# A two-layer encoder trunk on eight cores: LayerNorm by token tile under a contraction-outer head of the second pointwise projection, later relayout reads, and ten modulation blocks moved to the first FFN

## The chip, the cores and the metric

The kernel runs on the eight cores of one Trainium2 chip (two dies: cores 0 to 3 and 4 to 7). Every core does the same work on its own slice of the tokens (1184 columns), so every core streams all the weights. The metric is the device time of the slowest core, in microseconds (us). The time before the change is 3435.83 us (median of 3 runs, 3432.84 to 3686.82).

The highest of those three is not scatter. In some executions of any version of this program, the cores of one die (or of both) show a lower granted TensorE clock and take longer. Such runs are called slow here, the others fast, and only fast runs are compared.

A ratio below is the mean time of one kernel's fast runs over the mean time of the other's fast runs of the same rounds. The interval in brackets is the 95% interval. A verdict of faster or slower needs a difference of over 2%; it is unclear where the interval reaches across 2%.

## The reference, cut to what matters

```python
def conv_module(h, state, w_pw1, b_pw1, w_dw, b_dw, ln_g, ln_b, w_pw2, b_pw2):
    a, gt = jnp.split(h @ w_pw1 + b_pw1, 2, axis=-1)
    u = a * jax.nn.sigmoid(gt)                                   # GLU
    up = jnp.concatenate([state.astype(u.dtype), u], axis=1)
    z = lax.conv_general_dilated(up, w_dw[:, None, :]...) + b_dw # depthwise, width 31
    z = jax.nn.silu(layer_norm(z, ln_g, ln_b))                   # over the 2048 channels
    return z @ w_pw2 + b_pw2, up[:, T:]

def run_trunk(x, c, ...):
    for i in range(2):                       # layer 0: conv module, layer 1: window attention
        mod = jax.nn.silu(c) @ p['w_mod'][i] + p['b_mod'][i]
        sh1, sc1, g1, sh2, sc2, g2 = jnp.split(mod, 6, axis=-1)
        h = modulate(rms_norm(x, p['norm_mix'][i]), sh1, sc1)
        y = conv_module(...) or attention(...)
        x = x + g1[:, None, :] * y
        h = modulate(rms_norm(x, p['norm_ffn'][i]), sh2, sc2)
        x = x + g2[:, None, :] * swiglu(h, p['w_gu'][i], p['w_down'][i])
```

The six modulation vectors of a layer are 48 "mod blocks" of 256 columns: blocks 0 to 7 are `sh1`, 8 to 15 `sc1`, 16 to 23 `g1`, 24 to 31 `sh2`, 32 to 39 `sc2`, 40 to 47 `g2`. A mod block is a 1 MB weight block (2048 x 256 in bf16, cast from float32 on its way in) for 1 us of matmul work.

## The kernel before

All weights flow through a ring of four 1 MB slots in the order of one list, `plan`. A slot is refilled in strict order: block `i` only goes where block `i - 4` was, and only when that one is done.

```python
        for b in range(24, 32):
            wblock(f"mod0_{b}", wmod, b, KC)
        for b in range(8):
            wblock(f"pw2_{b}", wpw2, b, KC)
            for m in PW2M[b]:
                wblock(f"mod0_{m}", wmod, m, KC)
        # ... layer 1:
                wblock("q_0", wqkv, 0, KC)
                for b in range(16, 26):
                    wblock(f"mod1_{b}", wmod, 48 + b, KC)
                for b in range(1, 8):
                    wblock(f"q_{b}", wqkv, b, KC)
                    for x in range(2):
                        wblock(f"mod1_{24 + 2 * b + x}", wmod, 72 + 2 * b + x, KC)

        def ring_fill():
            while ring["next_pf"] < len(plan) and (ring["next_pf"] < NR or ring["next_pf"] - NR in ring["rel"]):
                ring_prefetch(ring["next_pf"])
                ring["next_pf"] += 1
```

The convolution needs another layout of its input than pw1 (the first pointwise projection) gives, and so does LayerNorm of the convolution's output. Both go through DRAM: write `ud`, read `ud`; write `zd`, read `zd`, all issued by SyncE (SP). SP works in program order, so a read that waits for its write holds up all that SP issues after it.

```python
                t_w = dma(SP, ud[c], US[:, c % 2, :], us_sem[c % 2])           # end of pw1 chunk c
                # ...
                SP.wait(t_w, vb_free[c % 2])
                vb_ready[c] = dma(SP, VB[:, c % 2, :, :], ud[c].rearrange(...), vb_sem[c % 2])
    # ... and in conv_chunk(c):
            t_w = dma(SP, zd[c].rearrange(...), ZS[:, b, :, :], zs_sem[b])
            # ...
            SP.wait(t_w)
            zc_ready[c] = dma(SP, ZC[:, c, :], zd[c], zc_sem[c])
```

Then come the statistics matmuls, eight mod blocks, LayerNorm on whole rows of 1184 tokens, chunk by chunk of the 16 channel chunks, and pw2 (the second pointwise projection) with its epilogue, with the contraction `k` innermost:

```python
        for cc in range(KC):
            DVE.emit(... ZC[:, cc, :] - MEAN)
            DVE.emit(... ZC[:, cc, :] * RSC)
            act(HB[:, cc, 32:1184]..., zv..., AF.Silu, scale=lg, bias=lb)      # cut
            xready0.append(dma(SP, X[:, cc, :], xv[:, cc, 32:NH], xr_sem[cc])) # x replaces z
    # proj_resid, for each of 16 output rows n and 3 token tiles t:
                        PE.wait(*bf[bk])                                       # bk: two banks in turn
                        for k in range(KC):
                            mm(PS[bk][:, 0:ncols], slot[:, k, 128 * h:128 * h + 128], rhs_of(k, xlo, ncols), ...)
                        ACT.wait(tp, tfree)
                        act(TMPE[...], PS[bk][...], AF.Identity, scale=g1, bias=G1B)   # cut
                        DVE.emit(... X[:, n, xlo:xlo + ncols] += TMPE[:, 0:ncols])
                        tfree = DVE.tick()
```

In attention the list puts ten mod blocks of layer 1 between `q_0` and `q_1`; they are used up while ScalarE computes the position bias, before the first scores.

The softmax here doesn't subtract the row's maximum and nothing guards it: scores larger than these inputs give would overflow.

## Time and profile before

The profile is of the slowest core, core 3. Its page starts with the span and the busy time of each engine and has, further on, the chain of waits followed back from the last instruction:

```profile
span 3435.6 us, 54718 instructions; the slowest of 8 cores (3396.2 to 3435.6 us)
...
PE 3001.0 (87%) x21988; PEld 1861.9 (54%) x21988; DVE 1136.0 (33%) x2591; ACT 717.0 (21%) x1321; POOL 187.3 (5%) x357
...
PE 74%; DMA 14%; DVE 4%; ACT 3%; issue 3%; SPq 1%; DVEq 0%; POOL 0%; ACTq 0%; POOLq 0%
```

TensorE (PE) is the limit, busy for 87% of the span. PE time by itself can't be cut by this change, so what counts are the stretches where PE stands still. The next view gives the busy time in chosen stretches of core 3: the stretch, its length, busy us of each engine with the number of instructions, the granted PE clock, the mean DMA share, GB/s.

```profile
core 3: us, PE busy (x) PEld busy (x) DVE busy (x) ACT busy (x) POOL busy (x), PEclk, DMA share, GB/s
165.00:517.00 352.00, 317.37 (x2352) 202.11 (x2352) 170.12 (x459) 45.85 (x66) 21.10 (x40) 0.95 0.79 155
...
553.00:604.00 51.00, 6.49 (x228) 6.17 (x225) 45.63 (x38) 33.07 (x40) 4.23 (x8) 0.52 0.98 187
...
1955.00:2047.00 92.00, 39.87 (x705) 28.42 (x706) 17.33 (x47) 35.02 (x32) 5.63 (x11) 0.65 0.64 115
2047.00:2225.00 178.00, 161.23 (x1760) 115.54 (x1760) 94.05 (x243) 93.38 (x193) 10.11 (x20) 0.93 0.67 127
```

Read the second column against the first. pw1 and the convolution (165 to 517) leave PE idle for 35 us; LayerNorm (553 to 604) leaves it idle for 44 of 51 us, while DVE is nearly full but the DMA engines (0.98) are full too; the start of attention (1955 to 2047) leaves it idle for 52 us. The list of all PE waits, by what ended them (us in total, times, longest):

```profile
PE ps L250 <- DMA RING<-wmod: 85.5, 20, 8.0
...
PE ps L250 <- DMA UBraw<-ud: 46.1, 5, 12.6
```

Single instructions of PE show where they are (start, length, what, and in brackets the idle time just before it and what ended it). The first is a convolution chunk waiting for its relayout read; the next is the first pw2 matmul, which waits for LayerNorm's output; the last two are waits for mod blocks in attention.

```profile
345.87 5.15 PE L250 MATMUL ps<-UBraw 128*128 128x156 bf16 x40 [12.64 <-DMA UBraw<-ud]
...
604.29 11.01 PE L250 MATMUL ps<-HBraw,RING 128*128 128x384 bf16 x48 [16.92 <-ACT HBraw L253]
...
2010.52 1.00 PE L250 MATMUL ps<-SCT,RING 128*128 128x3 bf16 x32 [8.05 <-DMA RING<-wmod]
...
2084.81 0.99 PE L250 MATMUL ps<-SCT,RING 128*128 128x3 bf16 x32 [2.75 <-DMA RING<-wmod]
```

Why a read comes late is seen in SP's own issues. Each line is one transfer handed over; SP is stuck between them:

```profile
276.23 0.38 SPq L245 DMA_DIRECT2D ud<-UBraw  x1
...
281.46 0.37 SPq L245 DMA_DIRECT2D UBraw<-ud  x1
281.93 0.52 SPq L245 DMA_DIRECT2D zd<-UBraw  x1
291.44 0.33 SPq L245 DMA_DIRECT2D Xraw<-zd  x1
291.88 0.76 SPq L245 DMA_DIRECT2D ud<-UBraw  x1
```

The write of `zd` at 281.93 has to land before its read is issued at 291.44, and only then does SP get to the next `ud` write at 291.88: two round trips through DRAM in one line.

A stage runs from the first PE matmul of one kind to the first of the next, read from each core's trace and averaged over the eight cores: pw1, statistics, pw2, FFN 0, the K and V projections, the first scores, the output projection wo, FFN 1. Before:

| stage (us, mean of 8 cores) | before |
|---|---|
| pw1 to statistics | 367.7 (358 to 382) |
| statistics to first pw2 matmul | 56.0 |
| pw2 to FFN 0 | 158.4 |
| FFN 0 to K/V | 1136.3 |
| K/V to first scores | 147.0 |
| first scores to wo | 224.3 |
| wo to FFN 1, and FFN 1 to the end | 129.3, 1035.2 |

### The profile page before, as it was taken

The numbers are of one execution on the slowest core, as the hardware profiler recorded it, in microseconds if no ns is written. First come the engines' busy times: TensorE is split into PE (matmuls) and PEld (weight loads), VectorE is DVE, ScalarE is ACT, GpSimd is POOL, SyncE is SP. The second block draws the span as 40 slices with busy tenths as digits, with TensorE's granted clock in tenths as the row PEclk, the third lists the DMA queues.
The fourth block names the chain that finished last, engine by engine and source line by source line (L and its number), as shares of the span: only waits on it lengthen the run. The fifth ranks groups of instructions, "written<-read, shape, count | busy, mean of one in ns | idle before, by whom it ended". The sixth has DMA issues, their size and how long they took to land.

```text
span 3435.6 us, 54718 instructions; the slowest of 8 cores (3396.2 to 3435.6 us)
## 1 busy us (share of the span) xinstructions
PE 3001.0 (87%) x21988; PEld 1861.9 (54%) x21988; DVE 1136.0 (33%) x2591; ACT 717.0 (21%) x1321; POOL 187.3 (5%) x357
## 2 busy tenths in 40 slices
PE   2298982998999999999999649889899999999996
PEld 0165652554556565555554336656566666666663
DVE  0344547123231413122134525542322222323136
ACT  2411114453000000000003635555300000000003
POOL 0000000000000000000000000000000000000000
PEclk9999995999999999999999869979899999999998
DMA  9787778953666565424245376654375353535343
GB/s 214 135 149 158 159 153 173 208 104 60 125 107 115 86 124 90 82 44 84 46 77 129 87 122 125 127 148 74 53 134 97 50 99 50 95 53 90 54 74 120
DMA packets 107111, 366.87 MB, mean 107 GB/s; under 512 B 31424, under 2 KB 51008, under 8 KB 77920
## 3 DMA queue, kind: packets, MB, share of 16 engines
q0 software_dynamic: 51024, 285.67, 47.8%
q1 hardware_dynamic: 55840, 77.70, 7.6%
q8 instruction: 180, 2.95, 0.4%
q14 instruction: 67, 0.55, 0.1%
HBM read 615.89 MB, written 33.78 MB: 189 GB/s over the span
## 4 chain that ended last, share of the span: by engine, by line
PE 74%; DMA 14%; DVE 4%; ACT 3%; issue 3%; SPq 1%; DVEq 0%; POOL 0%; ACTq 0%; POOLq 0%
PE ps L250 74%; DMA RING<-wmod 4%; DMA ud<-UBraw 3%; DMA zd<-UBraw 2%; DMA Xraw<-xT 1%; SPq L245 1%; ACT HBraw L253 1%; DMA RING<-wgu 1%; DMA UBraw<-ud 1%; DVE Xraw L884 1%; DVE Xraw L607 1%; DMA RING<-wpw 1%; ACT SCR L253 1%; DMA RING<-wqkv 1%; DVE UBraw L465 0%
## 5 line engine op out<-in xcount | busy, mean ns | idle before, releaser
L250 PE MATMUL ps<-HBraw,RING 128*128 128x352 bf16 (+2 forms) x11616 | 1944.2, 328 | 88.9 <-ACT HBraw L253 57.9
L250 PEld LDWEIGHTS ps<-HBraw,RING 128*128 128x128 bf16 x11616 | 1139.3, 99 | 823.6 <-issue 121.2
L250 PE MATMUL ps<-UBraw,RING 128*128 128x352 bf16 (+2 forms) x4992 | 812.5, 320 | 15.4 <-DVE UBraw L534 7.3
L250 PEld LDWEIGHTS ps<-UBraw,RING 128*128 128x128 bf16 x4992 | 472.7, 98 | 331.7 <-issue 65.1
L534 DVE TENSOR_TENSOR UBraw<-ps,SCR 128x352 bf16<-128x352 f32 (+2 forms) x264 | 144.0, 547 | 1170.9 <-PE ps L250 1166.9
L253 ACT ACTIVATE SCR<-ps 128x352 f32<-128x352 f32 (+2 forms) x264 | 126.8, 482 | 1812.6 <-PE ps L250 1812.6
L607 DVE SCALAR_TENSOR_TENSOR Xraw<-ps,MOD,Xraw 128x16 f32<-128x16 f32 (+3 forms) x960 | 395.3, 447 | 322.0 <-PE ps L250 321.9
L250 PE MATMUL ps<-SCT,RING 128*128 128x3 bf16 x3072 | 90.9, 165 | 131.0 <-DMA RING<-wmod 85.5
L250 PEld LDWEIGHTS ps<-SCT,RING 128*128 128x128 bf16 x3072 | 90.0, 98 | 144.1 <-issue 136.7
L250 PE MATMUL ps<-SCR,ONESB 128*128 128x352 bf16 (+2 forms) x240 | 80.0, 362 | 78.5 <-ACT SCR L253 78.5
L253 ACT ACTIVATE SCR<-Xraw 128x352 bf16<-128x352 f32 (+3 forms) x208 | 117.1, 565 | 120.6 <-DVE Xraw L511 66.9
L511 DVE TENSOR_TENSOR Xraw<-Xraw,SCR 128x352 f32<-128x352 f32 (+2 forms) x96 | 52.6, 548 | 221.2 <-ACT SCR L253 216.1
L253 ACT ACTIVATE Xraw<-Xraw 128x512 bf16<-128x512 f32 (+4 forms) x154 | 107.6, 720 | 51.8 <-DVE Xraw L1143 36.5
L245 POOL DMA_DIRECT2D RING<-wmod x96 | 50.9, 532 | 919.1 <-PE ps L250 806.6
L245 POOL DMA_DIRECT2D RING<-wdn x96 | 50.7, 528 | 891.5 <-PE ps L250 888.9
L250 PE MATMUL ps<-UBraw 128*128 128x156 bf16 x640 | 54.8, 254 | 48.5 <-DMA UBraw<-ud 46.1
L245 POOL DMA_DIRECT2D RING<-wgu x88 | 46.5, 529 | 888.1 <-PE ps L250 871.3
L253 ACT ACTIVATE SCR<-ps,G1B,MOD 128x16 f32<-128x16 f32 (+3 forms) x160 | 79.1, 536 | 75.8 <-PE ps L250 75.7
L1143 DVE SCALAR_TENSOR_TENSOR Xraw<-ps,Xraw 128x512 f32<-128x512 f32 x128 | 82.3, 685 | 36.1 <-PE ps L250 36.0
L250 PEld LDWEIGHTS ps<-SCR,ONESB 128*128 128x128 bf16 x240 | 23.2, 102 | 110.6 <-issue 102.5
L250 PEld LDWEIGHTS ps<-UBraw 128*128 128x128 bf16 x640 | 52.8, 109 | 51.8 <-issue 50.2
L745 DVE SCALAR_TENSOR_TENSOR UBraw<-ps,VTs,SCR 128x128 bf16<-128x128 f32 (+1 forms) x192 | 48.7, 316 | 92.1 <-PE ps L250 88.7
(90 smaller groups left out, 1026.2 us busy)
## 6 DMA issues: line engine op xcount, KB each, us to landing
RING<-wmod POOLq DMA_DIRECT2D x96, 1024.0 KB, 13.7
RING<-wgu POOLq DMA_DIRECT2D x88, 1024.0 KB, 8.7
RING<-wdn POOLq DMA_DIRECT2D x80, 512.0 KB, 5.2
RING<-wpw POOLq DMA_DIRECT2D x24, 1024.0 KB, 15.3
Xraw<-xT SPq DMA_DIRECT2D x32, 592.0 KB, 35.9
RING<-wqkv POOLq DMA_DIRECT2D x10, 1024.0 KB, 18.6
zd<-UBraw SPq DMA_DIRECT2D x16, 592.0 KB, 8.5
Xraw<-zd SPq DMA_DIRECT2D x16, 592.0 KB, 5.1
```

The costliest lines, as they stand in the source:

```text
L245: engw.e.dma_start(out=out, in_=in_).then_inc(sem, 16)
L250: return PE.emit(nc.tensor.matmul(out, lhsT=lhsT, rhs=rhs, start=start, stop=stop, **kw))
L253: return ACT.emit(nc.scalar.activation(out=out, in_=in_, func=func, **kw))
L511: DVE.emit(nc.vector.tensor_tensor(out=X[:, n, xlo:xlo + ncols], in0=X[:, n, xlo:xlo + ncols], in1=TMPE[:, 0:ncols], op=ALU.add))
L534: DVE.emit(nc.vector.tensor_tensor(out=ACTR[:, aslot, xlo:xlo + ncols], in0=PS[bu][:, 0:ncols], in1=SGF[:, i, 0:ncols], op=ALU.mult))
L607: DVE.emit(nc.vector.scalar_tensor_tensor(out=X[:, n, a:b_], in0=PS[bk][:, a - xlo:b_ - xlo], scalar=MOD[:, li, 80 + n, bi_:bi_ + 1], in1= ...
L745: DVE.emit(nc.vector.scalar_tensor_tensor(out=out, in0=i0, scalar=ba_s, in1=i1, op0=ALU.add, op1=ALU.mult))
L884: DVE.emit(nc.vector.tensor_tensor(out=ZC[:, cc, :], in0=ZC[:, cc, :], in1=MEAN, op=ALU.subtract))
L1143: DVE.emit(nc.vector.scalar_tensor_tensor(out=SS[:, 2 * w + half, :], in0=bank[:, :], scalar=0.125, in1=BIAS[:, 8 * a + 2 * ip + half, :], ...
```

## The change

It has four parts.

1. Relayout reads are issued later: the `ud` read of chunk `c` one tile into the next pw1 chunk, the `zd` read further on, so that SP isn't held up by a write that has only just been issued.
2. The ten mod blocks move from the start of attention into FFN 0.
3. The ring gets a list of free slots: the next block goes into whichever slot comes free first.
4. LayerNorm is applied by token tile (384, 384, 416 columns), with every second chunk's subtraction on GpSimd (Pool). pw2's first three weight blocks (six output rows) become a "head": for each token tile, `k` is the outer loop and six PSUM banks accumulate together, so that matmuls can start as soon as the first chunk of the first tile is normalized, and PE runs while LayerNorm goes on. The residual `x` of those six rows is staged early in buffers `XS`, since its home still holds `z`. Mod blocks 32 to 34 move into the head.

```diff
+        XS = [carve(UBraw, o, (128, NX), F32) for o in (0, 4736, 19712, 24448, 29184, 33920)]
-        PW2M = [[32, 33], [34], [35], [36], [37], [38], [39], []]
+        PW2M = [[], [], [32, 33, 34], [35, 36], [37], [38], [39], []]
-                for j in range(8, 24):
+                for j in range(8, 34):
                     fm[j] = [(1, j - 8)]
-                for b in range(16, 26):
-                    wblock(f"mod1_{b}", wmod, 48 + b, KC)
 ... (ring)
+            while ring["pf"] < len(plan) and ring["free"]:
+                s, tok = ring["free"].pop(0)
+                POOL.wait(tok)
+                ring["load"][i] = dma(POOL, RING[:, s, 0:nk, 0:ncols], src, slot_sem[s])
 ... (proj_resid)
+            if head is not None:
+                hs = [ring_use(f"{wname}_{b}") for b in range(3)]
+                apply(0)
+                for t, (xlo, ncols) in enumerate(tiles):
+                    if t == 1:
+                        apply(1, 8, KC)
+                    elif t == 2:
+                        apply(2, 8, KC)
+                    mods(li, [modp[2][t]], 6 + t % 2)()
+                    for bk in range(6):
+                        PE.wait(*bf[bk])
+                    for k in range(KC):
+                        PE.wait(kready[t, k])
+                        for n in range(6):
+                            mm(PS[n][:, 0:ncols], hs[n // 2][0][:, k, 128 * (n % 2):128 * (n % 2) + 128],
+                               rhs_of(k, xlo, ncols), k == 0, k == KC - 1)
+                    tp = PE.tick()
+                    if t < 2:
+                        apply(t + 1, 0, 8)
+                    for n in range(6):
+                        DVE.wait(xs_tok[n])
+                        epi(n, t, n, tp, xs[n])
+                        late.append((n, t))
 ... (pw1_tile, conv_chunk: the two reads go; the main loop gets)
+                if ti == 1 and c >= 1:
+                    vb_load(c - 1)
+                if ti == 2 and c >= 2:
+                    zc_load(c - 2)
 ... (LayerNorm)
+        for n in range(6):
+            xs_tok.append(dma(SP, XS[n], xv[:, n, 32:NH], xr_sem[n]))
+        def ln_apply(t, c0=0, c1=KC):
+            for cc in range(c0, c1):
+                if cc % 2:
+                    POOL.emit(nc.gpsimd.tensor_tensor(out=zt, in0=zt, in1=mv, op=ALU.subtract))
+                    DVE.wait(POOL.tick())
+                else:
+                    DVE.emit(nc.vector.tensor_tensor(out=zt, in0=zt, in1=mv, op=ALU.subtract))
+                    DVE.wait(DVE.tick())
+                DVE.emit(nc.vector.tensor_tensor(out=zt, in0=zt, in1=rv, op=ALU.mult))
+                ... Silu on ACT
-        mb()
-        barrier()
```

`epi` is the old epilogue as a function. ACT's program order: after tile `t`'s matmuls it first does half of the next tile's LayerNorm (`apply(t + 1, 0, 8)`), then the six epilogues, then the other half.

## The prediction

> **What bounds it now.** TensorE: 87% busy, 74% of the chain of waits. The FFNs run full at clock 1.00, so three stretches can pay (slowest core, core 3):
>
> 1. pw1 + conv, 165 to 517 us: PE 317 of 352 us, DMA share 0.79. The list of waits gives PE 46.1 us in 5 waits for the read of `ud`. SP runs write ud, wait, read, write zd, wait, read in one line (8 to 17 us each in the chain). After a stall a conv chunk takes 4.5 us, not 2.9: the Trainium skill ("TensorE: Matmul & The Clock Gate", Part 1) says an idle PE falls to half clock; windows with a stall show 0.73 to 0.83, which agrees.
> 2. LayerNorm, 553 to 604 us: PE 6 of 51 us; DVE, two 1.39 us passes per chunk, sets the pace, but DMA share is 0.98 too.
> 3. Attention start, 1955 to 2047 us: PE 40 of 92 us, seven waits for mod blocks of some 6 us each. Then, to 2225 us, six waits of 2 us: a slot is refilled in strict order behind the q block.
>
> **Costs.**
> - Later reads: four stalls (33 us on core 3) and their cold restarts (2 us each) go; the wait at the last chunk (12.6 us) stays. Core 3 gains 34 us, core 4 21, cores 1, 2, 5, 6 only 10 to 16. Slowest core: estimated -24 us.
> - Mod blocks: the last bias units run at ScalarE's 1.8 us, so the first scores start near 2010, not 2047: -37, and -2.6 for the q_1 wait. The free list ends the six waits (12.5 us) and their restarts: -24. In FFN 0 a group with 8 mods takes 199.7 us, without 193.7: +7.5 for ten. Sum -56.
> - LayerNorm head: before its first tile PE needs mod28 to mod31, three pw2 blocks and mod32, all loaded after 553 us. A block takes 5.9 us at full DMA, an x chunk 2.3 us. Eight blocks, six staged x chunks and one z chunk are 63 us from 547: PE starts near 610, not 604. DVE and Pool also wait for mod31. In the head, half a tile of LayerNorm waits behind six serial epilogues (1.4 us each): 5 to 10 us. After it, ten x chunks, six copies and three blocks compete, and pw2_4 comes 5 to 15 us late. Pool's subtract is some 0.85 us per 384 columns, an estimate from the Trainium skill ("GPSIMD Engine Reference", 3.1: 4497 ns for 2048 columns; before's trace has no such op), so it doesn't bind. Net: +15 us (0 to +28) against the 51 that seem on offer.
>
> Total: -24 - 56 + 15 = -65; leaning late on the head, 3374 us.
>
> **Range** 3345 to 3403. Faster by over 2%: 0.38; same: 0.60; slower: 0.02.
>
> **Checks.** Right if: PE waits for `ud` reads fall to one or two, at the last chunks; no mod waits in attention, which is about 60 us shorter; FFN 0 about 7 us longer; the first pw2 matmul comes about 60 us after the convolution statistics, ended by a ring block, at DMA share 1.0; gaps between the head's tiles; a wait for a pw2 block after the head.
>
> **Wrong if:** DMA is faster and pw2 starts well before 600 (then 3340); pw1, shortened, meets the DMA limit (0.79 of 352 is 278 us of 310) and stalls anew; Pool's subtracts are several times slower or slow DVE (then 3400).

## More of the kernel before

One buffer, `TMPE`, sits between ScalarE (ACT) and VectorE (DVE): the epilogue of one bank can't start before DVE has read the one before it. Here that costs nothing, since PE works 2.8 us on each bank.

## The result, and the profile after

The fast runs of the change took 3391.5 and 3388.66 us (median of all four runs 3437.8, two being slow: 3667.27 and 3484.09), against 3435.76 for the kernel before (median of four, one slow). The ratio of fast runs is 0.987 [0.9841, 0.9898]: 1.3% faster. 3390 lies inside the predicted range, 16 us above the predicted 3374.

After, the profile is of core 5, a fast run (cores 3368.9 to 3390.4 us, clock 0.953 to 0.958 on both dies). The page:

```profile
span 3390.4 us, 54940 instructions; the slowest of 8 cores (3368.9 to 3390.4 us)
...
PE 2989.5 (88%) x21988; PEld 1853.8 (55%) x21988; DVE 1152.2 (34%) x2631; ACT 721.3 (21%) x1353; POOL 210.9 (6%) x381
...
PE 82%; DMA 6%; DVE 4%; ACT 4%; issue 3%; SPq 1%; DVEq 0%; POOL 0%; ACTq 0%; POOLq 0%
```

DMA's part of the chain of waits fell from 14% to 6%. PE's waits in total:

```profile
PE ps L251 <- ACT SCR L254: 109.9, 26, 38.3
...
PE ps L251 <- DMA RING<-wmod: 75.5, 10, 20.9
...
PE ps L251 <- DMA UBraw<-ud: 11.2, 1, 11.2
```

The `ud` waits have gone from five (46.1 us) to one (11.2 us), which stands at the last chunk, as predicted; every other core also has exactly one, 10.7 to 14.1 us. The waits for mod blocks, however, are down by only 10 us. Between 1850 and 2250 us the list of PE's instructions has no wait for a DMA any more, so they have to be elsewhere. They are in front of the head, as the list of PE's instructions there shows, from the statistics to the end of the head:

```profile
508.97 4.10 PE L251 MATMUL ps<-SCR,MP 128*128 128x148 bf16 x32 [8.94 <-DVE SCR L899]
...
529.79 0.99 PE L251 MATMUL ps<-SCT,RING 128*128 128x3 bf16 x32 [13.50 <-DMA RING<-wmod]
...
555.10 1.00 PE L251 MATMUL ps<-SCT,RING 128*128 128x3 bf16 x32 [7.07 <-DMA RING<-wmod]
576.98 0.99 PE L251 MATMUL ps<-SCT,RING 128*128 128x3 bf16 x32 [20.88 <-DMA RING<-wmod]
577.83 9.75 PE L251 MATMUL ps<-HBraw,RING 128*128 128x384 bf16 x48
588.70 7.96 PE L251 MATMUL ps<-HBraw,RING 128*128 128x384 bf16 x48 [1.11 <-ACT HBraw L254]
...
608.26 17.69 PE L251 MATMUL ps<-HBraw,RING 128*128 128x384 bf16 x96 [10.82 <-ACT SCR L254]
...
634.00 19.75 PE L251 MATMUL ps<-HBraw,RING 128*128 128x416 bf16 x96 [7.26 <-ACT SCR L254]
655.18 5.36 PE L251 MATMUL ps<-HBraw,RING 128*128 128x384 bf16 x32 [1.43 <-ACT SCR L254]
667.84 0.48 PE L251 MATMUL ps<-SCR,ONESB 128*128 128x384 bf16 x1 [7.30 <-ACT SCR L254]
```

The first pw2 matmul comes at 577.83, 68.9 us after the statistics; before, 56.0 us after them. Up to 577 PE waits for ring blocks: 13.50 us for the first, some 7 us for each of the next three, and then 20.88 us, during which three pw2 blocks and mod block 32 come in. Then the head runs, and after each of its three tiles comes a gap (10.82, 7.26 and 7.30 us, the third after two more banks of pw2). Each is ended by ACT's work on `SCR`, the area that holds the epilogue's buffer `TMPE` (and, for the third, the squares for the next norm). The five gaps after 577.83 sum to 1.11 + 10.82 + 7.26 + 1.43 + 7.30 = 27.9 us. PE also restarts slowly after them: the bank after the 7.30 us gap takes 5.72 us, the next ones 2.76 to 2.98.

The stretches of core 5 that answer to those of before: the first begins with pw1 and ends 31.3 us ahead of the statistics, as the stretch 165 to 517 does; the second runs from the statistics to the head.

```profile
166.60:477.70 311.10, 310.48 (x2352) 195.62 (x2352) 170.52 (x462) 45.14 (x63) 21.33 (x41) 1.00 0.88 175
509.00:577.00 68.00, 11.29 (x289) 11.01 (x290) 25.27 (x21) 8.62 (x13) 19.45 (x24) 0.53 0.98 197
578.00:690.00 112.00, 84.08 (x555) 47.52 (x554) 53.99 (x91) 58.83 (x113) 13.07 (x17) 0.85 0.59 150
```

In the first, the same 2352 matmuls take 311 us instead of 352, PE is idle for under 1 us instead of 35, and DMA share rose from 0.79 to 0.88. In the second, PE works 11 of 68 us at a DMA share of 0.98. In the third, PE works 84 of 112 us.

The stage table shows where the time went on the mean core:

| stage (us, mean of 8 cores) | before | after | difference |
|---|---|---|---|
| pw1 to statistics | 367.7 (358 to 382) | 342.3 (341 to 343) | -25.4 |
| statistics to first pw2 matmul | 56.0 | 68.3 | +12.3 |
| pw2 to FFN 0 | 158.4 | 185.5 | +27.1 |
| FFN 0 to K/V | 1136.3 | 1144.9 | +8.6 |
| K/V to first scores | 147.0 | 113.7 | -33.3 |
| first scores to wo | 224.3 | 200.8 | -23.5 |
| wo to FFN 1, and FFN 1 to the end | 129.3, 1035.2 | 129.7, 1036.0 | +1.2 |
| end of the mean core | 3416.9 | 3383.1 | -33.8 |
| end of the slowest core | 3435.6 | 3390.4 | -45.2 |

Three parts gave what was expected of them and the head gave the opposite: statistics to FFN 0 grew by 39.4 us. The slowest core gained more than the mean core, because before, the cores differed by 24 us in pw1 and now they differ by 2.

Two views say what fills the gaps in the head. This is ACT around the first one and at the start of the second (Silu of LayerNorm writes `HBraw`, an epilogue reads `ps` and writes `SCR`):

```profile
599.12 1.30 ACT L254 ACTIVATE HBraw<-Xraw,VTs 128x384 bf16<-128x384 f32 x2 [0.29 <-DVE Xraw L953]
600.33 0.65 ACT L254 ACTIVATE SCR<-ps,G1B,MOD 128x384 f32<-128x384 f32 x1
601.74 0.67 ACT L254 ACTIVATE SCR<-ps,G1B,MOD 128x384 f32<-128x384 f32 x1 [0.76 <-DVE UBraw L503]
...
607.45 0.67 ACT L254 ACTIVATE SCR<-ps,G1B,MOD 128x384 f32<-128x384 f32 x1 [0.76 <-DVE UBraw L503]
...
626.05 0.67 ACT L254 ACTIVATE SCR<-ps,G1B,MOD 128x384 f32<-128x384 f32 x1 [2.06 <-PE ps L251]
```

Tile 0's matmuls end at about 596.6 (588.70 + 7.96). ACT is at that time in the first half of tile 1's LayerNorm and comes to the first epilogue at 600.33. There are six, one every 1.43 us, though ACT works only 0.67 us on each: the idle 0.76 us before each is ended by DVE's add (line 503), which frees `TMPE`. The first matmuls of tile 1 need all six banks, because with `k` outermost every bank takes part in every step, so PE starts at 608.26. At the second gap ACT is not late: it has waited 2.06 us for PE when its first epilogue starts at 626.05, so the 7.26 us are the six epilogues alone. The 3.5 us more of the first gap come from ACT's late start, and e5 below shows where that comes from.

The other thing in the head was not expected at all. DVE's multiply on line 953 takes 0.54 us, except twice, where Pool's subtractions (line 947) run:

```profile
557.30 16.00 DVE L953 TENSOR_TENSOR Xraw<-Xraw,UBraw 128x384 f32<-128x384 f32 x2
...
573.87 1.03 DVE L953 TENSOR_TENSOR Xraw<-Xraw,UBraw 128x384 f32<-128x384 f32 x2
...
578.67 9.55 DVE L953 TENSOR_TENSOR Xraw<-Xraw,UBraw 128x384 f32<-128x384 f32 x2
```

And Pool in the same time:

```profile
557.18 15.22 POOL L947 TENSOR_TENSOR Xraw<-Xraw,UBraw 128x384 f32<-128x384 f32 x16
...
579.12 8.21 POOL L947 TENSOR_TENSOR Xraw<-Xraw,UBraw 128x416 f32<-128x416 f32 x8
```

While Pool goes through 16 subtractions back to back (557.18 to 572.40), one DVE multiply that started at 557.30 stays in flight for 15.53 us (the line joins it with the next one: 16.00 us for two). The Trainium skill, "SBUF — State Buffer", section "Who interferes with whom", says that a DVE instruction with two SBUF inputs contends with a GpSimd instruction that reads SBUF, through a shared port pair that is locked for a whole instruction. The trace agrees. A lock for one instruction would not give 15.53 us, since each subtraction takes only 0.98 us; but each of Pool's records starts about 0.03 us before the one before it ends, so the trace shows no free moment between them (times on Pool are rough). Whether it costs time is tested below.

### The profile page after: what moved, and what is told of

The parts are those of the page before. It is cut to its first block, busy times and chain, and to the rows that moved or that the text cites. A ratio compares the mean times of both kernels' runs of the same rounds, so it can differ in the third digit from the quotient of the medians.

```text
span 3390.4 us, 54940 instructions; the slowest of 8 cores (3368.9 to 3390.4 us)
## 1 busy us (share of the span) xinstructions
PE 2989.5 (88%) x21988; PEld 1853.8 (55%) x21988; DVE 1152.2 (34%) x2631; ACT 721.3 (21%) x1353; POOL 210.9 (6%) x381
## 4 chain that ended last, share of the span: by engine, by line
PE 82%; DMA 6%; DVE 4%; ACT 4%; issue 3%; SPq 1%; DVEq 0%; POOL 0%; ACTq 0%; POOLq 0%
PE ps L251 81%; DMA RING<-wmod 2%; ACT HBraw L254 2%; DMA Xraw<-xT 1%; DMA RING<-wgu 1%; SPq L246 1%; ACT SCR L254 1%; DVE SCR L466 1%; ACT Xraw L254 1%; DVE Xraw L645 0%; DVE UBraw L466 0%; DMA ud<-UBraw 0%; ACT UBraw L254 0%; DVE Xraw L1211 0%; DVE UBraw L1352 0%
## 5 line engine op out<-in xcount | busy, mean ns | idle before, releaser
L254 ACT ACTIVATE SCR<-Xraw 128x352 bf16<-128x352 f32 (+2 forms) x190 | 107.6, 568 | 106.6 <-DVE Xraw L503 55.6
L503 DVE TENSOR_TENSOR Xraw<-Xraw,SCR 128x352 f32<-128x352 f32 (+2 forms) x78 | 42.3, 542 | 176.0 <-ACT SCR L254 176.0
L254 ACT ACTIVATE SCR<-ps,G1B,MOD 128x384 f32<-128x384 f32 (+3 forms) x160 | 79.1, 535 | 75.5 <-PE ps L251 63.1
L254 ACT ACTIVATE SCR<-ps,VTs 128x416 f32<-128x416 f32 (+2 forms) x64 | 36.1, 570 | 174.0 <-PE ps L251 173.8
L254 ACT ACTIVATE HBraw<-UBraw,MOD,AM 128x16 bf16<-128x16 f32 (+2 forms) x108 | 61.0, 635 | 49.1 <-DVE UBraw L701 38.8
```

The source lines that it names most:

```text
L254: return ACT.emit(nc.scalar.activation(out=out, in_=in_, func=func, **kw))
L503: DVE.emit(nc.vector.tensor_tensor(out=dst[:, xlo:xlo + ncols], in0=dst[:, xlo:xlo + ncols], in1=TMPE[:, 0:ncols], op=ALU.add))
```

## The experiments

**Theory.** Reads, moved blocks and the free list are worth what was predicted, some 80 us together. The head costs some 40 us, from two things: its start is late, because the staged `x` transfers and the blocks of the head share the DMA engines, and its tiles turn over slowly, because six serial epilogues stand between two tiles. **Rivals.** (a) One of the other parts gave less than predicted. (b) The head's loss is the exclusion of DVE by Pool. (c) The head is bound by the total work of ACT and DVE, so that no repair of its order wins LayerNorm's 51 us.

All outputs are right.

### e1_nohead: the change without the head

```diff
- ln_apply by token tile, XS, the head of proj_resid, PW2M with 32 to 34 in the head
+ LayerNorm, barrier and proj_resid call of the kernel before
+ PW2M = [[32, 33], [34], [35], [36], [37], [38], [39], []]
```

> The change without its LayerNorm head (the LayerNorm and the pw2 loop of before, with the later reads, the free list and the moved mod blocks). Theory: the head itself costs time; by the stages of the two traces (mean of 8 cores) pw2 starts 12 us later after the statistics and its stretch is 27 us longer, so this kernel is some 39 us faster than the changed one, near 3350 us (ratio to before 0.975), with statistics to pw2 at 56 us and pw2 to FFN at 158 us again. Rival: the head hides a cost that comes back without it (a shortened pw1 pushes DMA work into this stretch); then it is within 10 us of the changed kernel, near 3390 us.

Measured: 3353.0 us, median of three fast runs, ratio to before 0.9748 [0.9724, 0.9771]. (The profiled run had die 0 slow, but the stages quoted here hardly differ between the dies: the longest is within 3.2 us of the mean.) Statistics to pw2 is again 56.0 us, pw2 to FFN 0 158.7, K/V to scores 112.9, scores to wo 201.1. The three other parts are worth 2.5%, and the head takes about half of it back: 0.987 against 0.9748 is 1.2%, some 42 us, which agrees with the 39.4 us of the stage table. The two ratios come from different rounds, so this is a cross-check, not a second measurement.

### e2_reads_only: only the later reads, on the kernel before

```diff
-                SP.wait(t_w, vb_free[c % 2])
-                vb_ready[c] = dma(SP, VB[:, c % 2, :, :], ud[c]...)
 ... (likewise the zd read)
+                if ti == 1 and c >= 1:
+                    vb_load(c - 1)
+                if ti == 2 and c >= 2:
+                    zc_load(c - 2)
```

> Before with the later relayout reads alone. Theory: pw1 to statistics falls from 368 us (mean of 8 cores, 353 to 382) to 342 us on every core and nothing else moves, so the slowest core is some 25 us faster, near 3410 us (0.993). Rival: the gain in pw1 needs the free list (which also serves the pw1 blocks); then pw1 stays above 355 us.

Measured: 3408.3 us, ratio 0.9906 [0.9875, 0.9937]. pw1 to statistics is 343.3 us on the mean core instead of 367.7; all other stages are within 3.5 us of before. The reads alone are worth 0.94%, 32 us, somewhat more than the predicted 24, though the interval (22 to 43 us) includes 24. What e1 has beyond e2 is 0.9906 - 0.9748 = 1.6%, 54 us, for the moved blocks with the free list, where 56 was predicted. Rival (a) falls.

### e3_mods_strict: only the moved blocks, with the strict ring

```diff
-                for j in range(8, 24):
+                for j in range(8, 34):
-                for b in range(16, 26):
-                    wblock(f"mod1_{b}", wmod, 48 + b, KC)
 (and the ten mods() calls before the first scores go)
```

> Before with the ten mod blocks moved to the first FFN, but with the old strictly ordered ring. Theory: the move alone shortens K/V to first scores from 147 to 114 us and lengthens FFN 0 by 8 us, while first scores to wo stays at 224 us, since that stall is the ring's order; total -25 us, near 3411 us. Rival: the move also ends the stalls in the attention loop (fewer blocks in the ring); then first scores to wo falls to 201 us here as well, total -48 us, near 3388 us.

Measured: 3411.4 us, ratio 0.9933 [0.9868, 0.9998]. K/V to scores fell to 113.3 us, but scores to wo stayed at 220.7 (before 224.3), and the waits for mod blocks in attention are still there:

```profile
2098.12 0.99 PE L250 MATMUL ps<-SCT,RING 128*128 128x3 bf16 x32 [2.83 <-DMA RING<-wmod]
```

So the moved blocks shorten the stretch before the first scores, and the free list the stretch after it (220.7 to 201.1 in e1, which adds the later reads too; these alone left it at 224.7 in e2). The free list without the move was not run.

### e4_split: the head with three banks at a time

The six banks of a tile are split in two groups of three, each with its own pass over `k`; the epilogues of one group run while PE is in the other.

```diff
-                    for k in range(KC):
-                        for n in range(6):
+                    for g in range(2):
+                        for k in range(KC):
+                            for n in range(3 * g, 3 * g + 3):
 (half of the next tile's LayerNorm and three epilogues after each group)
```

> The changed kernel with each token tile of the head done as two passes of three output rows (banks 0 to 2, then 3 to 5), half a tile of LayerNorm emitted after each. Theory: the two gaps of 10.8 and 7.3 us between the head's tiles are all six banks changing over at once behind six serial epilogues; with two sets of three banks the gaps fall under 3 us each and pw2 to FFN falls from 185 us to about 168, total near 3373 us. Rival: LayerNorm on DVE and ACT, or the DMA queue, paces the head; then PE waits for HB chunks in place of the epilogues and the time stays within 5 us of the changed kernel, near 3390 us.

Measured: 3389.2 us, ratio 0.9858 [0.9826, 0.9889]. pw2 to FFN 0 went from 185.5 to 177.0 us where 168 was expected. On the slowest core the gaps between groups are 2.76, 2.33 and 2.61 us, so the turnover did shrink, but a wait of 4.93 us for LayerNorm output in the first tile (one DVE subtraction is in flight for 8.87 us there, beside eight of Pool's) and 3.01 us at the end remain. The whole time can't tell 8 us from the change itself (0.987); the stage can.

### e5_dve_only: the subtraction on DVE only

```diff
-                if cc % 2:
-                    POOL.emit(nc.gpsimd.tensor_tensor(out=zt, in0=zt, in1=mv, op=ALU.subtract))
-                else:
-                    DVE.emit(nc.vector.tensor_tensor(out=zt, in0=zt, in1=mv, op=ALU.subtract))
+                DVE.emit(nc.vector.tensor_tensor(out=zt, in0=zt, in1=mv, op=ALU.subtract))
```

> The changed kernel with all LayerNorm subtracts on DVE, none on Pool. In the changed kernel's trace one DVE multiply of 0.54 us takes 15.5 us, exactly while Pool runs 16 subtracts back to back, and another 9.1 us during 8 more. Theory: the two engines exclude each other there; without Pool no DVE operation of this stretch takes over 1 us; but most of that block lies under the wait for ring blocks, and DVE now has 0.3 us more per chunk, so pw2 to FFN changes by under 6 us either way and the time stays near 3390 us. Rival: the block of 25 us is on the critical path and is most of the head's loss; then the time falls by 15 us or more, to 3375 us or less.

Measured: 3396.6 us, ratio 0.9858 [0.9829, 0.9887]; pw2 to FFN 0 is 185.1 us (after: 185.5), statistics to pw2 67.3 (68.3). Without Pool, every DVE multiply of the first tile takes 0.56 us and the 15.5 us record is gone. The exclusion is real, but in the change most of it is off the critical path: PE is waiting for mod block 32 until 577 us anyway. The second block, of 9.1 us from 578.67, is not: it makes ACT late for the first epilogue, and without Pool the first gap is as long as the second was:

```profile
610.07 18.52 PE L251 MATMUL ps<-HBraw,RING 128*128 128x384 bf16 x96 [7.27 <-ACT SCR L254]
```

On the slowest core the head's gaps are 7.27, 8.85, 1.43 and 7.30, some 3 us shorter in sum, but its stage is only 2.6 us shorter than that of the change's slowest core (185.4 and 188.0 us), and in the mean of the cores it is the same. Rival (b), that the exclusion is most of the head's loss, falls.

### e6_xs_late: the staged `x` after the head's ring blocks

```diff
-        for n in range(6):
-            xs_tok.append(dma(SP, XS[n], xv[:, n, 32:NH], xr_sem[n]))
+        def xs_issue():
+            SP.wait(PE.tick())                     # the head's first mod block is used
+            for n in range(6):
+                xs_tok.append(dma(SP, XS[n], xv[:, n, 32:NH], xr_sem[n]))
 (called in the head, at t == 0)
```

> The changed kernel with the six staged x chunks requested only when PE starts the head's first tile, not at the end of the convolution. Theory: these 3.6 MB stand in front of the ring blocks that PE waits for, so the first block after the statistics comes in 7 us in place of 13.5, and the first pw2 matmul follows the statistics by about 58 us in place of 68: 8 to 10 us faster, near 3382 us. Rival: the blocks' own bandwidth or the Pool-blocked LayerNorm sets that start; then it stays at 66 us or more and the time at 3390 us.

Measured: statistics to pw2 59.2 us (after 68.3, before 56.0), pw2 to FFN 0 185.0; whole time 3387.7 us, ratio 0.9832 [0.9803, 0.9861]. PE's waits for the ring blocks after the statistics, on the slowest core:

```profile
548.88 0.99 PE L251 MATMUL ps<-SCT,RING 128*128 128x3 bf16 x32 [7.78 <-DMA RING<-wmod]
555.54 0.99 PE L251 MATMUL ps<-SCT,RING 128*128 128x3 bf16 x32 [5.67 <-DMA RING<-wmod]
...
591.98 0.99 PE L251 MATMUL ps<-SCT,RING 128*128 128x3 bf16 x32 [22.34 <-DMA RING<-wmod]
```

The first wait is 7.78 us instead of 13.50 and the next three 5.2 to 5.9 instead of 7.1 to 7.8: the six transfers of `x` stood among the blocks that PE waits for. They cost 9 of the 12 us by which the head started later. The last wait, for three pw2 blocks and mod block 32, is still 22 us.

### e7_late2: the head at once, mod blocks later

Rival (c) is tested by a head that doesn't wait for blocks it has no need of. Mod blocks 24 to 31 (`sh2`) are first needed in FFN 0. The first three pw2 blocks are loaded ahead of all of them; five mod blocks run between the groups of the head, the others in the rest of pw2. It also has the groups of three and no Pool.

```diff
-        for b in range(24, 32):
-            wblock(f"mod0_{b}", wmod, b, KC)
+        for b in range(3):
+            wblock(f"pw2_{b}", wpw2, b, KC)
+        for m in [24, 25, 26, 27, 28]:
+            wblock(f"mod0_{m}", wmod, m, KC)
-        PW2M = [[], [], [32, 33, 34], [35, 36], [37], [38], [39], []]
+        PW2M = [[], [], [], [29, 30], [31, 32, 33], [34, 35], [36, 37], [38, 39]]
```

> A version meant to beat both: head in two passes of three banks, subtracts on DVE, and the eight mod blocks 24 to 31 (shift of the FFN's norm, needed only there) taken out of the front of the head and spread over pw2, so that the ring holds the first three pw2 blocks when the statistics come. Theory: the head's start was bound by eight ring blocks; now pw2 starts 12 to 15 us after the statistics, paced by LayerNorm (about 1.1 us per chunk and 1.4 us per epilogue, 65 us for the head), and the FFN starts 170 to 195 us after the statistics (253 in the changed kernel, 214 without the head): 3310 to 3330 us. Rival: the DMA work only moves (20 blocks, 16 x chunks and 6 copies are about 170 us) and PE meets it again as waits for blocks behind the head; then the FFN starts over 205 us after the statistics and the time is near that without the head, 3350 us.

Measured: 3367.4 us, ratio 0.9787 [0.9757, 0.9817]; pw2 starts 12.5 us after the statistics, but FFN 0 starts 12.5 + 213.4 = 226 us after them. With no head (e1) it is 56.0 + 158.7 = 215 us. The rival was right about the stage; the whole time, 17 us above 3350, is by the 2% rule unclear. Four lines of PE on the slowest core, from the first tile to the end of pw2:

```profile
528.35 0.65 PE L251 MATMUL ps<-HBraw,RING 128*128 128x384 bf16 x3 [0.48 <-ACT HBraw L254]
...
579.80 9.81 PE L251 MATMUL ps<-HBraw,RING 128*128 128x416 bf16 x42 [5.90 <-ACT SCR L254]
...
608.00 6.98 PE L251 MATMUL ps<-HBraw,RING 128*128 128x384 bf16 x32 [3.11 <-DMA RING<-wpw]
...
737.68 7.64 PE L251 MATMUL ps<-HBraw,RING 128*128 128x384 bf16 x36 [13.41 <-DVE SCR L469]
```

In the first pass PE does three matmuls (0.65 us) and waits 0.48 us for the next normalized chunk; until 539 us DVE is busy for 14.7 of 16.2 us, so LayerNorm sets the pace. In the later tiles LayerNorm shares ACT and DVE with the epilogues (5.90 us). The head takes from 522.8 to 605, some 82 us, in which PE is busy for 63 us, DVE for 56 and ACT for 51: over the whole head no engine is full, and PE waits now for one, now for the other. At the full rate the eighteen banks would take some 48 us (2.60 us a bank of 384 columns, 2.81 of 416, an estimate from the undisturbed part of pw2). DMA share is 0.69 in the head, and afterwards blocks come late (PE waits 3.11 us for the first, and 11 us more in four waits further on); FFN 0 waits 13.41 us at the end (5.43 in the change).

### e8_repaired: e4, e5 and e6 together

```diff
 e4's groups of three + e5's DVE only + e6's xs_issue
```

> The changed kernel with three repairs at once and the plan of blocks unchanged: two passes of three banks, subtracts on DVE, x chunks requested late. Theory: the three causes account for the head's loss of 39 us, so the FFN starts about 215 us after the statistics (253 in the changed kernel) and the time equals that of the kernel without the head, 3350 us, not better, since eight ring blocks still come first. Rival: something else in the head costs time; then it stays above 3365 us.

Measured: fast runs 3374.7 and 3380.9 us, ratio 0.9806 [0.9768, 0.9844], by the 2% rule unclear. The profiled run: its cores 2 to 5 show the lower clock only after 2960 us, and on them statistics to FFN 0 is 232 to 240 us, 235 in the mean. The change has 254, e1 215: the three repairs win back 19 of 39 us, not all. The expectation, that it would equal e1, was missed. The trace says what is left: on core 5 PE still waits for ACT five times in the head and just after it (2.23, 6.08, 0.51, 2.97 and 3.02 us, 14.8 in sum). e7 and e8 both keep the single buffer `TMPE`, and no run joined e9's two buffers to them; so rival (c), that no repair of the order can win LayerNorm's time, is neither shown nor ruled out.

### e9_epi2: the change with two epilogue buffers

```diff
-                ACT.wait(tp, st["tfree"])
-                    act(TMPE[...], PS[bk][...], ...)
+                e = st["e"] % 2; st["e"] += 1
+                TE = (TMPE, T1[:, 0, :])[e]
+                ACT.wait(tp, st["tfree"][e])
+                    act(TE[...], PS[bk][...], ...)
```

> The changed kernel with two alternating epilogue buffers (the second in the norm's scratch), so that ScalarE's scaling of one output overlaps DVE's add of the one before. Theory: the head is held up by its serial epilogues, 18 of 1.4 to 2.0 us on ScalarE and DVE in turn; at about 0.8 and 1.2 us each the gaps between tiles fall from 10.8 and 7.3 us to about 7 and 4, the one after the head from 7.3 to about 3: pw2 to FFN from 185 to about 173 us, total near 3378 us. Rival: LayerNorm work on the same two engines, not the epilogues, sets those gaps; then they stay within 2 us and the time near 3390 us.

Measured: 3399.7 us, ratio 0.9856 [0.9829, 0.9882]; on this chip the kernel before took 3450.0 us and die 0 ran at a lower clock (0.951), so the total says little. The stage says it: pw2 to FFN 0 is 172.4 us instead of 185.5 (171.4 on the four undisturbed cores of die 1). The three gaps on the slowest core:

```profile
613.53 17.57 PE L251 MATMUL ps<-HBraw,RING 128*128 128x384 bf16 x96 [7.30 <-ACT SCR L254]
...
635.44 19.83 PE L251 MATMUL ps<-HBraw,RING 128*128 128x416 bf16 x96 [3.56 <-ACT SCR L254]
...
664.89 0.38 PE L251 MATMUL ps<-SCR,ONESB 128*128 128x384 bf16 x1 [2.83 <-ACT SCR L254]
```

10.82, 7.26 and 7.30 us became 7.30, 3.56 and 2.83. With the two small ones (0.17 and 1.43) they sum to 15.3 us instead of 27.9: 12.6 us less, and the stage is 13.1 us shorter in the mean of the cores. So 13 of the 27 us by which this stage grew are the serial handing-over of one buffer.

### e10_chunk_head: another head, on e1

e7 suggests to let LayerNorm run at its own speed on whole rows, as before, and give PE something to do beside it. Six banks are two output rows times three token tiles, so the first pw2 block can be accumulated chunk by chunk as LayerNorm delivers chunks. No staged `x` is needed. The first pw2 block goes ahead of mod blocks 24 to 31, which run in between; epilogues have two buffers.

```diff
             zapp[cc] = ACT.tick()
+            PE.wait(zapp[cc])
+            for n in range(2):
+                for t, (xlo, ncols) in enumerate(tilesX):
+                    mm(PS[3 * n + t][:, 0:ncols], slot0[:, cc, 128 * n:128 * n + 128],
+                       HB[:, cc, 32 + xlo:32 + xlo + ncols], cc == 0, cc == KC - 1)
+            if cc % 2 == 0 and 2 <= cc <= 10:
+                evs.append(mods(0, [26 + cc // 2], 7, 8 * (2 + cc // 2), False))
```

> The kernel without the head, but with the first pw2 block (two output rows by three tiles, six banks) accumulated chunk by chunk while the whole-row LayerNorm runs, the mod blocks 24 to 31 interleaved between those steps, and the two epilogue buffers. Theory: LayerNorm has 2.8 us per chunk and these matmuls need 1.0, so an eighth of pw2 (16 us) is done under LayerNorm at no cost in epilogues except one change of six banks (about 5 us): statistics to FFN 200 to 205 us in place of 214, total near 3338 us, faster than the changed kernel and than the one without a head. Rival: the DMA queue (20 blocks and 16 x chunks, about 155 us at full rate after the statistics) paces the stretch; then waits for pw2 blocks appear behind the head and the FFN starts at 212 us or later, 3350 us.

Measured: 3369.6 us, median of five fast runs, ratio 0.9768 [0.9738, 0.9797], on the chip where the kernel before took 3450.0. Statistics to FFN 0 is 15.1 + 188.2 = 203 us (201 on the undisturbed die 1), as expected, against 215 without a head and 254 in the change. The expected total, 3338 us, was missed: in the profiled run the undisturbed die 1 took 3328 to 3338 us, but die 0, at a lower clock (0.952), up to 3369. The chunk head, the moved blocks and the second buffer were not tested apart. Its ratio can't be told from e1's 0.9748 of another chip.

### e11_nohead_b and e12_chunk_head_b: e1 and e10 on one chip

No edit; the same two kernels.

> The kernel without the head again, beside the next one on one chip, because the two were timed on different chips so far (0.9748 against 0.9768, intervals overlapping) although the stage from statistics to FFN is 12 us shorter in the other. Expected: ratio near 0.975 again, statistics to FFN 214 to 215 us.

> The chunk-by-chunk head again, on the same chip as the kernel without a head. Theory: the stage of 203 us against 215 us is what counts, and the earlier ratio was spoilt by a die at lower clock; then it is 8 to 14 us (0.3%) faster than the run beside it. Rival: the denser stretch lowers the granted clock elsewhere or moves waits to a later stage; then the two are equal within 3 us, and the later stages are longer by 10 us.

Measured: die 1 was slow in nearly all runs of this chip, so there is no ratio of fast runs. The undisturbed die 0 can still be read: the slowest of its four cores took 3349.6 to 3360.4 us without a head (ten runs, median about 3356) and 3339.7 to 3352.6 with the chunk head (five runs, median about 3348; the profiled run, where cores 2 and 3 of this die were disturbed too, is left out). By the medians that is about 8 us for the chunk head, the low end of what was expected, and the stages are 216 and 203 us. The gain is plain in the stages and small in the total; on the whole program it is not settled.

## Why the prediction was right or wrong

The total was right to 16 us, and within its range, but that was in part luck: the head's +39 us lies outside the prediction's own 0 to +28 for it, and the later reads gave more than was predicted, so that two misses were of opposite sign.

- **Later reads: right, a little low.** Predicted -24 us on the slowest core; e2 alone measured -32. Every core gained (16 to 40 us where 10 to 34 had been put down), and all reach the statistics within 341 to 343 us of pw1's start. One wait, at the last chunk, stayed, as predicted. The fear that pw1 would meet the DMA limit didn't come true (share 0.88, PE idle for under 1 us of 311). The cold restarts that the prediction took from the Trainium skill, "TensorE: Matmul & The Clock Gate", Part 1 (an idle PE falls to half clock), are in the trace: before, the convolution chunk after the 12.64 us stall takes 5.15 us, and the one at 519.27 us, after 2.40 us of idling, 2.88 us.
- **Mod blocks and free list: right.** Predicted -56 in sum; e1 less e2 is 54 us. By stages: -33.3 (-37 - 2.6 predicted) before the scores, -23.5 (-24) after them, +8.6 (+7.5) in FFN 0. e3, with e2, showed that the free list is what ended the waits after the first scores.
- **The head: the mis-sized term.** Predicted "+15 (0 to +28)"; it measured +39.4 us in the stages, and 42 by ratios. The parts, as the prediction put them:
  - *"PE starts near 610, not 604"*, +6 us: counted from the statistics it starts 12.3 us later than before. e6 shows 9 us of them to be the staged `x` among the ring blocks. The prediction had these transfers in its sum of 63 us, so here only the size was off, by 6 us.
  - *"half a tile of LayerNorm waits behind six serial epilogues (1.4 us each): 5 to 10 us"*: the 1.4 us were right (1.43), but the wait was looked for at the wrong place and once. It is PE that waits, after each of the three tiles: a tile with `k` outermost can't start before all six banks of the one before are emptied (10.82 and 7.26 us), and after the third the next banks stand behind its six epilogues (7.30). That is 27.9 us with the small gaps. In the mean of the cores PE's idle time in this stage grew by 22 us (11.5 to 33.5), and its busy time for the same matmuls by 5 (147 to 152), which goes with a lower granted clock (0.90 on the slowest core in this stage, 0.97 before): together the +27.1. e9 shows 13 of them to be the single buffer, and e5 that 3.5 us of the first gap came from Pool. The Trainium skill says it in "Perfetto Trace Analysis", section "Optimizing Tensor Performance" (Matmuls): independent groups should rotate through banks so that the evacuation of one overlaps the matmuls of the next. Six banks in lockstep don't, and the 7.26 us of the second gap are the number for it; before, with two banks in turn, pw2 has no such gap from one bank to the next.
  - *"pw2_4 comes 5 to 15 us late"*: it didn't; the trace has no wait for a pw2 block after the head.
  - *Pool "doesn't bind"*: right for the time (e5), but not for the reason given, its speed. Pool's 16 subtractions take 15.22 us, 0.95 each for 384 columns, near the 0.85 estimated from the Trainium skill's "GPSIMD Engine Reference" (3.1), so the speed was about right. That Pool might slow DVE stood only among the signs that would prove the prediction wrong, at 3400 us; it did slow it, by 15 and 9 us, and this was mostly hidden, because the head starts late. In e4 it is not: PE waits 4.93 us for LayerNorm in the first tile, and e8, which has e4's groups without Pool, has no such wait on cores 2 to 5 (its `x` is late too, so this was not tested alone).

LayerNorm left PE idle for 44 us, and the prediction rightly doubted that these were on offer, but not enough. A head in token tiles can only use them if its weights are there, and DMA share was 0.98 in this very stretch. And when the blocks are there (e7), PE waits for ACT and DVE in the head and for late blocks after it. The chunk-by-chunk form (e10) gets 12 us of those 44; it adds no LayerNorm instruction and no transfer of `x`, and moves only matmuls and their blocks (beside the second epilogue buffer).

## What to carry to other kernels

Before an idle stretch is filled, ask which other engine is full in it; here DMA (share 0.98) was, and DVE nearly (45.6 of 51 us), and the head gave both more to do there. If several banks accumulate in lockstep, count the time from the last matmul to the *last* bank emptied as PE idle time at every tile's end, and look at what the evacuating engine has queued before it. A change of several parts should be measured part by part: here three parts were worth 2.5%, and the fourth took half of it away without the total showing it.

## What the Trainium skill lacked or had wrong

- "SBUF — State Buffer" ("Who interferes with whom") has the lock of the shared ports, and that the two engines exclude each other agrees. It lacks that a run of GpSimd instructions can keep DVE out for the whole run: one DVE multiply (0.54 us alone) was in flight for 15.5 us beside 16 back-to-back subtractions, and a second one some 9 us beside 8.
- "GPSIMD Engine Reference" (3.1) gives 4497 ns for 2048 columns. Scaled down, that is 0.85 us for 384 columns; the trace has 0.95 us (15.22 us for 16), so scaling by columns is a tenth low here.
- No page was found that says how fast a 1 MB weight block arrives that is cast on the way while others load (there are bandwidth limits, but no such time): here one came every 6.2 to 6.9 us with the `x` transfers out of the way (e6, from the first matmul on one block to the first on the next) and every 8.1 to 8.8 us beside them (the change), and this set the head's start.
- "TensorE: Matmul & The Clock Gate" (Part 1) has a limiter that takes the whole die to 13/16 of the clock. The records of the slow cores have that value (0.81, beside the 1.0 and 0.5 that all cores have), but not for a whole die: in the profiled run of e12 cores 2 and 3 have six stretches of 15.1 us at it and cores 0 and 1 of the same die none; in that of e1 cores 2 and 3 have it for some 370 us from 164 us on, cores 0 and 1 only from 3026 us on. The page lacks that such stretches come in some executions of a program and not in others.
